# The first rows of a prefix log-sum-exp: found by Relu passes, or loaded apart

## The chip, the cores and the metric

The kernel runs on one core of a Trainium2 chip. The metric is device time in microseconds of one launch: 1260.91 us as the median of three runs before the change (1260.88 to 1261.64). One further execution was recorded by the hardware profiler; its span is 1258.4 us, from the first to the last instruction. The engines of the core are called PE (TensorE, matmul), ACT (ScalarE, activation functions), DVE (VectorE), POOL (GpSimd) and SP (SyncE, which here issues transfers). Sixteen DMA engines move the data between the memory of the chip and the core's own buffers.

## What is computed

The input is `x` of shape (4, 4096, 4128), float32, drawn from a normal distribution. For each of the 4 batches and 4128 columns, the output at row t is the logarithm of the sum of exp over rows 0 to t:

```
out[:, 0, :] = x[:, 0, :]
for t in range(1, S):
    mx = max(out[:, t-1, :], x[:, t, :])
    out[:, t, :] = mx + log(exp(out[:, t-1, :] - mx) + exp(x[:, t, :] - mx))
```

270.5 MB are read and as many are written.

## The kernel before, in words

The kernel computes exp, running sums and log without the running maximum. This is exact enough as long as the values are moderate. A check that runs along decides at the end whether they were; if not, a slow general loop (`_general`) does everything again. The check has two parts. Each batch's last sum must not be too large (`probe`, at most 2^62). And the first rows must not be too small, since a first row alone has no other term to hold its sum away from zero: this part is what changes.

**Steps.** A batch's 4096 rows are cut into steps of 128 x r rows, r being 2 or 3 (`begin`, `usual`, `final`, lines 149 to 151). Partition p of a step holds r consecutive rows of 4128 columns. There are 49 steps, numbered through all batches; 13 belong to batch 0 and 12 to each of the others. They use four buffers in turn (`slots`), one of two rows and three of three. A load moves 4128 or 6192 KB, a store the same.

**Chunks.** A step's columns are cut into three chunks of 1376 (`CH`). For each chunk:

- `exp` (line 102): Exp in place over all r rows, on ACT. At the first step of a batch a second pass follows (line 105): Relu of (2^-63 - exp(x)) over row 0, one partition, whose sum along the row goes into one element of `short`. The sum is over zero if a value is smaller than 2^-63.
- `sums` (lines 114 and 116): DVE adds the rows of a partition, into `z`.
- `head` (line 124): PE multiplies `z` by a triangular matrix (`below` at a batch's first step, `carried` after it), so that each partition gets the sum of those above it.
- `add` (lines 133, and 141 or 136): DVE adds this to the rows. In the last step of a batch the `z` pass also writes a column of `probe`.
- `log` (lines 146 and 147): Ln in place, on ACT.

**Order.** Each engine has a list written out by hand: ACT takes the three Exps of step 0, then for each chunk the two Ln passes of step t and an Exp of step t + 1; DVE and PE follow suit. `moves` is the list of SP, which issues all 98 loads and stores: four loads, store 0, store 1, load 4, store 2, load 5 and so on. A load waits for the store that last used its buffer, a store for the step's Ln passes, and each stands in SP's queue behind the transfer before it. An engine executes its list in order.

**Completion counters.** Each transfer that SP or ACT issues adds to one of eight completion counters, which the framework deals out in turn, in the order in which it has put the transfers; whoever needs the data waits on the counter. SP's and ACT's transfers share these eight. A transfer that takes a counter again waits, in the queue of the engine that issues it, until that counter's last transfer has landed. In the program before, SP is the only issuer (but for `_general`), and eight transfers back is always long done.

**The begin.** POOL clears and builds the small constants (lines 44 to 65) and clears `z` (line 69). ACT loads its function table (line 34).

**The end.** Lines 236 to 251 fill `fits`, 1 where a value is in bounds: 12 columns for `probe`, then 12 in which partition 0 takes the comparison of `short`. DVE takes the minimum along each partition (`low`), PE sums over the partitions (`good`), DVE compares with 128 and writes `flag`, which every engine then loads and branches on (lines 254 and 255).

Of the kernel before, what the change touches and what calls it, by code (L numbers as in the profile page):

```python
# [7 lines left out]
FP32 = mybir.dt.float32  # L8
I32 = mybir.dt.int32
ACT = mybir.ActivationFunctionType  # L10
ALU = mybir.AluOpType
AX = mybir.AxisListType
P = 128
MM = 512
NC = 3
SLOTS = 4
SMALL = 2.0 ** -63
LARGE = 2.0 ** 62


# [1 line left out]
def kernel(  # L22
# [5 lines left out]
    nc = tc.nc  # L28
    B, S, D = x.shape
    assert S % P == 0 and D % (NC * 32) == 0  # L30
    CH = D // NC
# [3 lines left out]
    consts = ctx.enter_context(tc.tile_pool(name="consts", bufs=1))  # L35
# [10 lines left out]
        out=below, in_=below, pattern=[[1, P]], compare_op=ALU.is_ge,  # L46
# [5 lines left out]
        out=carried, in_=below, pattern=[[0, P]], compare_op=ALU.not_equal,  # L52
# [5 lines left out]
    probe = consts.tile([P, B * NC], FP32, name="probe")  # L58
    nc.gpsimd.memset(probe, 1.0)

    short = consts.tile([1, B * NC], FP32, name="short")
    spare = consts.tile([1, CH + 8], FP32, name="spare")[:, :CH]
    tiny = consts.tile([1, 1], FP32, name="tiny")
    nc.gpsimd.memset(short, 0.0)
    nc.gpsimd.memset(tiny, SMALL)

    z = [zpool.tile([P, CH], FP32, name=f"z{c}") for c in range(NC)]
    for t in z:
# [2 lines left out]
    slots = [x2.tile([P, 2, D], FP32, name="x0")]  # L71
    slots += [x3.tile([P, 3, D], FP32, name=f"x{k}") for k in range(1, SLOTS)]
    sides = [ppool.tile([P, CH], FP32, name=f"p{k}") for k in range(2)]

    ctx_sched = tc.manual_schedule()
    ctx_sched.__enter__()
# [16 lines left out]
    class Chunk:  # L93
# [3 lines left out]
            self.cols = slice(c * CH, (c + 1) * CH)  # L97

        def exp(self):
            t = self.t  # L100
            e = t.xt[:, :, self.cols]
            nc.scalar.activation(e, e, ACT.Exp)  # L102
            if t.first:
                k = t.b * NC + self.c
                nc.scalar.activation(  # L105
                    spare, t.xt[0:1, 0, self.cols], ACT.Relu, bias=tiny, scale=-1.0,
                    accum_out=short[:, k:k + 1],
                )

        def sums(self):  # L110
            r = self.t.r
# [108 lines left out]
    done, at = set(), {e: 0 for e in lists}  # L220
    while any(at[e] < len(l) for e, l in lists.items()):
        before = len(done), sum(at.values())
        for e, l in lists.items():
            while at[e] < len(l):
                op = l[at[e]]
# [7 lines left out]
        assert before != (len(done), sum(at.values()))  # L233


    fits = consts.tile([P, 2 * B * NC], FP32, name="fits")
    nc.vector.memset(fits[:, B * NC:], 1.0)
    nc.vector.tensor_scalar(
        out=fits[:, :B * NC], in0=probe, scalar1=LARGE, scalar2=None, op0=ALU.is_le,
    )  # L240
    nc.vector.tensor_scalar(
        out=fits[0:1, B * NC:], in0=short, scalar1=0.0, scalar2=None, op0=ALU.is_le,
    )
    low = consts.tile([P, 1], FP32, name="low")
    nc.vector.tensor_reduce(out=low, in_=fits, op=ALU.min, axis=AX.X)  # L245
# [4 lines left out]
        out=flag, in0=good, scalar1=float(P), scalar2=None, op0=ALU.is_lt,  # L250
# [62 lines left out]
```

## Time and profile before

| What | us |
|---|---|
| median of three runs | 1260.91 |
| span of the profiled execution | 1258.4 |
| DVE busy | 956.2 (76%) |
| ACT busy | 955.4 (76%) |
| PE busy | 602.4 (48%) |
| ACT waiting for loads (line 102) | 219.7, 43 times |
| DVE waiting for ACT's Exp (line 114) | 216.5, 35 times |
| load, issue to landing: 3 rows, 2 rows (median) | 38.4, 33.0 |
| store, issue to landing: 3 rows, 2 rows (median) | 25.0, 21.6 |

The profiled execution is one of its own; its span of 1258.4 us lies 2.5 us under the median, since the span counts from the first to the last instruction. The page shows busy time by engine, then the span cut into 40 slices of 31.5 us with each engine's busy share in tenths, the share of time that the DMA engines were at work, and the rate. A group line names the source line, the engine, the operation and its operands, the count, then busy time and mean duration in ns, then the idle time ahead of it. A time line gives the start, the duration, the engine, the line, and in brackets how long the engine sat idle before and what ended that. A row of busy time by stretches gives the stretch, its length, then busy time and count for PE, its weight loads, DVE, ACT and POOL, then the granted clock of PE, the share of the DMA engines' time that packets took (by the packets that start in the stretch, so that it can exceed 1), and GB/s.

### The profile page before, as it was taken

Reading aid. Unit: us, or ns where it says so; the run is one execution under the profiler, and the core shown is the slowest. Engines: PE = TensorE matmul, PEld = TensorE weight load, DVE = VectorE, ACT = ScalarE, POOL = GpSimd, SP = SyncE. Lnnn points to the kernel's source line nnn. Section 1 sums busy time; section 2 is a strip of 40 time slices with the busy share of each in tenths; the row PEclk is TensorE's granted clock in tenths of the full one; section 3 lists DMA queues with packets and bytes.
Section 4 is the critical chain, followed back from the end, with each engine's and each line's share of the span. In section 5 each row is a group of like instructions: output and inputs, shape, how many; then the busy total and the mean of one; then the engine's idle time right before and its main releaser. Section 6 shows DMA issues by size and latency. Waiting matters only on the chain.

```text
span 1258.4 us, 3228 instructions
## 1 busy us (share of the span) xinstructions
PE 602.4 (48%) x884; PEld 233.1 (19%) x884; DVE 956.2 (76%) x548; ACT 955.4 (76%) x466; POOL 4.6 (0%) x14
## 2 busy tenths in 40 slices
PE   3654454453535455345364535634535553463361
PEld 1221121121212122112121212211211211121120
DVE  3997696795967699579596679957957976795792
ACT  6987687786976699578697668866968966896792
POOL 1000000000000000000000000000000000000000
PEclk9877776676677667666676666766766776676676
DMA  9999999999999999999999999999999999999998
GB/s 403 420 439 426 432 436 428 432 437 429 439 425 438 430 437 433 436 435 427 440 422 436 436 432 434 434 430 435 437 428 437 431 435 431 434 437 433 432 435 354
DMA packets 14131, 541.28 MB, mean 430 GB/s; under 512 B 1568, under 2 KB 1568, under 8 KB 1568
## 3 DMA queue, kind: packets, MB, share of 16 engines
q1 hardware_dynamic: 14112, 541.07, 99.6%
q8 instruction: 7, 0.11, 0.0%
q14 instruction: 12, 0.10, 0.0%
HBM read 270.53 MB, written 270.53 MB: 430 GB/s over the span
## 4 chain that ended last, share of the span: by engine, by line
DMA 69%; ACT 14%; DVE 13%; PE 1%; issue 1%; SPq 0%; ACTq 0%; DVEq 0%
DMA x<-in_x_dram 52%; DMA out_dram<-x 17%; ACT x L102 6%; DVE x L133 5%; ACT x L146 5%; DVE z L116 3%; ACT x L147 3%; DVE z L141 3%; DVE x L114 2%; PE p L124 1%; SPq L91 0%; DVE z L136 0%; ACTq L146 0%; ACTq L254 0%; SPq L88 0%
## 5 line engine op out<-in xcount | busy, mean ns | idle before, releaser
L124 PE MATMUL p<-z,carried 128*128 128x512 f32 (+1 forms) x810 | 551.8, 842 | 544.3 <-DVE z L116 544.3
L102 ACT ACTIVATE x<-x 128x4128 f32<-128x4128 f32 (+1 forms) x147 | 468.0, 3187 | 219.7 <-DMA x<-in_x_dram 219.7
L124 PEld LDWEIGHTS p<-z,carried 128*128 128x128 f32 x810 | 213.4, 280 | 882.2 <-DVE z L116 648.3
L133 DVE TENSOR_TENSOR x<-p,x 128x2752 f32<-128x2752 f32 (+1 forms) x147 | 361.9, 2462 | 6.2 <-PE p L124 6.2
L146 ACT ACTIVATE x<-x 128x2752 f32<-128x2752 f32 (+1 forms) x147 | 300.6, 2045 | 63.5 <-DVE z L141 58.5
L114 DVE TENSOR_TENSOR x<-x 128x1376 f32<-128x1376 f32 x90 | 142.9, 1588 | 216.5 <-ACT x L102 216.5
L116 DVE TENSOR_TENSOR z<-x 127x1376 f32<-127x1376 f32 x147 | 233.9, 1591 | 53.8 <-ACT x L102 49.4
L141 DVE TENSOR_TENSOR z<-x 128x1376 f32<-128x1376 f32 x135 | 215.0, 1592 | 4.6
L147 ACT ACTIVATE x<-z 128x1376 f32<-128x1376 f32 x147 | 196.0, 1334 | 0.0
L124 PE MATMUL p<-z,below 128*128 128x512 f32 (+1 forms) x72 | 50.4, 864 | 87.4 <-DVE z L116 87.4
L124 PEld LDWEIGHTS p<-z,below 128*128 128x128 f32 x72 | 19.6, 289 | 117.7 <-DVE z L116 78.8
L136 DVE CUSTOM_DVE_ANT_0 z<-x 128x1376 f32<-128x1376 f32 x12 | 19.1, 1592 | 0.4
L105 ACT ACTIVATE spare<-x,tiny 1x1376 f32<-1x1376 f32 x12 | 17.3, 1442 | 0.5
L69 POOL MEMSET z<- 128x1376 f32 x3 | 3.7, 1241 | 0.0
L105 ACT ACTIVATION_READ_ACCUMULATOR spare<-x,tiny 1x1 f32 x12 | 2.2, 186 | 0.0
L247 PE MATMUL good<-ones,low 128*1 128x1 f32 x2 | 0.2, 164 | 3.8 <-DVE low L245 3.8
L34 ACT ACT_TABLE_LOAD x1 | 1.3, 1283 | 0.8 <-PEq L297 0.8
L136 DVE DVE_READ_ACCUMULATOR2_ANT probe<- 128x1 f32 x12 | 1.0, 83 | 0.0
L247 PEld LDWEIGHTS good<-ones,low 128*1 128x1 f32 x2 | 0.1, 80 | 4.8 <-DVE low L245 4.8
L249 DVE TENSOR_SCALAR flag<-good 1x1 int32<-1x1 f32 x1 | 0.1, 148 | 0.3 <-PE good L247 0.3
L51 POOL TENSOR_SCALAR_AFFINE_SELECT carried<-below 128x128 f32<-128x128 f32 x1 | 0.3, 290 | 0.0
L45 POOL TENSOR_SCALAR_AFFINE_SELECT below<-below 128x128 f32<-128x128 f32 x1 | 0.3, 285 | 0.0
(13 smaller groups left out, 1.6 us busy)
## 6 DMA issues: line engine op xcount, KB each, us to landing
x<-in_x_dram SPq DMA_DIRECT2D x30, 6192.0 KB, 38.4
out_dram<-x SPq DMA_DIRECT2D x30, 6192.0 KB, 25.0
x<-in_x_dram SPq DMA_DIRECT2D x19, 4128.0 KB, 33.0
out_dram<-x SPq DMA_DIRECT2D x19, 4128.0 KB, 21.6
```

Source lines behind the costliest of these rows:

```text
L34: nc.scalar.preload_act_table_set("natural_log_exp_and_others")
L69: nc.gpsimd.memset(t, 0.0)
L102: nc.scalar.activation(e, e, ACT.Exp)
L105: nc.scalar.activation(spare, t.xt[0:1, 0, self.cols], ACT.Relu, bias=tiny, scale=-1.0, accum_out=short[:, k:k + 1],)
L114: nc.vector.tensor_tensor(out=e[1], in0=e[0], in1=e[1], op=ALU.add)
L116: nc.vector.tensor_tensor(out=self.z[0:n], in0=e[r - 2][0:n], in1=e[r - 1][0:n], op=ALU.add,)
L124: nc.tensor.matmul(pt[:, a:b], lhsT=w, rhs=self.z[:, a:b], start=True, stop=True,)
L133: nc.vector.tensor_tensor(out=e, in0=base, in1=e, op=ALU.add)
L136: nc.vector.tensor_tensor_reduce(out=self.z, in0=ends[0], in1=ends[1], scale=1.0, scalar=0.0, op0=ALU.add, op1=ALU.add, accum_out=probe[:, ...
L141: nc.vector.tensor_tensor(out=self.z, in0=ends[0], in1=ends[1], op=ALU.add)
L146: nc.scalar.activation(e, e, ACT.Ln)
L147: nc.scalar.activation(t.xt[:, r - 1, self.cols], self.z, ACT.Ln)
```

## The change

The Relu passes and their tiles (`short`, `spare`, `tiny`) go. In their place, a tile `firsts` of 16 partitions, nine blocks of 129 numbers wide, is cleared by POOL at the begin and filled by 14 loads that ACT issues, ahead of everything else that ACT does but its table load. A batch's first row of 4128 numbers is 32 pieces of 129 numbers (516 bytes); the 14 loads take 2 to 15 such pieces each, one piece to a partition, and are packed into the blocks. At the end DVE takes the least value of each of the 16 partitions of `firsts`, and `fits` gets one column in which these are compared with -43. The tile is made 245 numbers wider than it is used. Exp's own passes, the steps, the lists and all loads and stores of SP stay as they are.

```diff
-SMALL = 2.0 ** -63
+LOWEST = -43.0
+ROWS = 16
+BLOCKS = 9
+PIECE = 129
+PAD = 245
+PARTS = [[15, 14, 3], [13, 12, 7], [11, 10, 9, 2], [8, 6, 5, 13]]
...
-    short = consts.tile([1, B * NC], FP32, name="short")
-    spare = consts.tile([1, CH + 8], FP32, name="spare")[:, :CH]
-    tiny = consts.tile([1, 1], FP32, name="tiny")
-    nc.gpsimd.memset(short, 0.0)
-    nc.gpsimd.memset(tiny, SMALL)
+    firsts = consts.tile([ROWS, BLOCKS * PIECE + PAD], FP32, name="firsts")[:, :BLOCKS * PIECE]
+    nc.gpsimd.memset(firsts, 0.0)
...
+    used = [0] * BLOCKS
+    for b, sizes in enumerate(PARTS):
+        assert sum(sizes) * PIECE == D
+        at = 0
+        for k in sizes:
+            g = next(g for g in range(BLOCKS) if used[g] + k <= ROWS)
+            nc.scalar.dma_start(
+                out=firsts[used[g]:used[g] + k, g * PIECE:(g + 1) * PIECE],
+                in_=x[b, 0, at * PIECE:(at + k) * PIECE].rearrange("(p f) -> p f", f=PIECE),
+            )
+            used[g] += k
+            at += k
...
-            if t.first:
-                k = t.b * NC + self.c
-                nc.scalar.activation(
-                    spare, t.xt[0:1, 0, self.cols], ACT.Relu, bias=tiny, scale=-1.0,
-                    accum_out=short[:, k:k + 1],
-                )
...
-    fits = consts.tile([P, 2 * B * NC], FP32, name="fits")
+    fits = consts.tile([P, B * NC + 1], FP32, name="fits")
...
+    least = consts.tile([ROWS, 1], FP32, name="least")
+    nc.vector.tensor_reduce(out=least, in_=firsts, op=ALU.min, axis=AX.X)
     nc.vector.tensor_scalar(
-        out=fits[0:1, B * NC:], in0=short, scalar1=0.0, scalar2=None, op0=ALU.is_le,
+        out=fits[0:ROWS, B * NC:], in0=least, scalar1=LOWEST, scalar2=None, op0=ALU.is_ge,
     )
```

More of the change, by code (lines that the diff above doesn't have):

```diff
@@ L99, in exp @@
         def exp(self):
-            t = self.t
-            e = t.xt[:, :, self.cols]
+            e = self.t.xt[:, :, self.cols]
             nc.scalar.activation(e, e, ACT.Exp)
-            if t.first:
-                k = t.b * NC + self.c
-                nc.scalar.activation(
-                    spare, t.xt[0:1, 0, self.cols], ACT.Relu, bias=tiny, scale=-1.0,
-                    accum_out=short[:, k:k + 1],
-                )
         def sums(self):
```

## The prediction

> **What bounds the kernel now.** I read the page's head and its DMA rows first.
>
> ```profile
> span 1258.4 us, 3228 instructions
> DVE  3997696795967699579596679957957976795792
> ACT  6987687786976699578697668866968966896792
> DMA  9999999999999999999999999999999999999998
> q1 hardware_dynamic: 14112, 541.07, 99.6%
> DMA 69%; ACT 14%; DVE 13%; PE 1%; issue 1%; SPq 0%; ACTq 0%; DVEq 0%
> ```
>
> ACT (ScalarE) and DVE (VectorE) are each 76% busy and have room in every slice; the 16 DMA engines have none in any. The one queue q1 moves 541.07 MB in the 1258.4 us, and its packets fill 99.6% of the engines' time. ACT and DVE appear in the chain of waits because a load that comes before its ACT pass is a step of that chain; that does not mean they limit the rate. The busy time by stretches says where DMA time is lost (last two columns: mean busy share of the DMA engines, GB/s):
>
> ```profile
> 0.00:12.00 12.00, 0.00 (x0) 0.00 (x0) 0.00 (x0) 1.28 (x1) 4.64 (x14) 1.00 0.87 352
> 12.00:47.60 35.60, 21.56 (x38) 8.95 (x39) 27.32 (x18) 33.87 (x23) 0.00 (x0) 0.90 1.01 424
> 100.00:1180.00 1080.00, 517.76 (x741) 199.24 (x739) 828.57 (x464) 820.01 (x390) 0.00 (x0) 0.67 1.00 433
> 1250.00:1258.40 8.40, 0.00 (x0) 0.00 (x0) 0.00 (x0) 0.00 (x0) 0.00 (x0) 0.50 0.35 150
> ```
>
> From 12 to 1250 us nothing is lost; 541.07 MB at 433 GB/s are 1249.6 us, so only 1258.4 - 1249.6 = 8.8 us lie around the saturated stream: start-up, a little below 433 GB/s early on, and an end in which the engines finish unevenly (share 0.35 over the last 8.4 us: 2.9 us of work for the mean engine, the rest is waiting for the last ones). The median of 1260.91 is 2.5 us above this span; I carry that 2.5 us over unchanged.
>
> **The passes that go.** 12 Relu passes on ACT, each with the read of its sum:
>
> ```profile
> L105 ACT ACTIVATE spare<-x,tiny 1x1376 f32<-1x1376 f32 x12 | 17.3, 1442 | 0.5
> L105 ACT ACTIVATION_READ_ACCUMULATOR spare<-x,tiny 1x1 f32 x12 | 2.2, 186 | 0.0
> ```
>
> 17.3 + 2.2 = 19.5 us of ACT time, three passes (4.9 us) at the first step of each batch. For batches 1 to 3 they lie inside the stretch where the DMA share is 1.00: stores would be issued some us sooner into a queue that still has a transfer running. Gain 0. The cover is the transfer in flight: SP stands a whole transfer ahead there (in one first step the ACT stream runs on from the Relu at 641.4, and the next pass that waits for a load starts at 647.0). For batch 0 the time line shows what follows:
>
> ```profile
> 13.07 2.50 ACT L102 ACTIVATE x<-x 128x2752 f32<-128x2752 f32 x1 [10.99 <-DMA x<-in_x_dram]
> 15.67 1.44 ACT L105 ACTIVATE spare<-x,tiny 1x1376 f32<-1x1376 f32 x1
> 22.35 1.59 DVE L133 TENSOR_TENSOR x<-p,x 128x1376 f32<-128x1376 f32 x1 [1.06 <-PE p L124]
> 25.60 1.35 ACT L146 ACTIVATE x<-x 128x1376 f32<-128x1376 f32 x1 [0.49 <-DVE z L141]
> 38.04 15.04 SPq L91 DMA_DIRECT2D out_dram<-x  x2
> 58.05 0.34 SPq L88 DMA_DIRECT2D x<-in_x_dram  x1
> ```
>
> The first Ln at 25.60 waits for DVE, DVE for PE's six matmuls from 17.41, and these for the first Exp alone. Without Relu the Exps end at 20.5 instead of 23.6, ACT idles until 25.6, and store 0 still goes out at 38.04. Gain 0 again. So all 19.5 us become ACT idle time: **0**.
>
> **The loads that come.** 14 loads, 128 rows of 516 bytes, 0.066 MB. By bytes, 0.066 MB / 433 GB/s = 0.15 us. By packets, no row shows one of 516 bytes. The page's instruction queue moved 12 packets beside the big ones in the trace: an 8192-byte one took 0.31 us (27 bytes per ns, so no visible fixed part), the 4-byte ones 0.01. So 0.02 to 0.1 us each, 8 on the mean engine and at most 14 on one (a load in which that engine has a share): 0.15 to 1.4 us, of which only what falls on the engine that ends last counts, so the low end is 0. I take **0.3**, near the byte rate, since the 8192-byte row already runs at it.
>
> The page DMA: Bandwidth & Descriptors of the Trainium skill (section "Why a DMA increments its semaphore by 16 and not by 1") says that a load from SP or ACT runs on the lowest-numbered k engines, k the largest divisor up to 16 of the slowest dimension. By it, k would be the partition count here, engine 0 would get 14 packets and engine 15 none, and the bound of 1.4 is right; with 8 on each it would be 0.8 and the low end 0.15. No row of before tells the engines apart.
>
> **What the loads delay.** ACT issues them ahead of its first Exp. They wait for GpSimd's clear of the new tile (16x1161; by the 1376-wide clear of 1.24 us, 1.05 us, ending near 2.1, no later than ACT's table load at 2.08). SP's four issues in a row took 1.91 us, 0.48 each, so 14 take 6.7 us: 2.1 + 6.7 = 8.8, ahead of 13.07 when load 0 lands. That alone costs nothing. But SP's and ACT's transfers share eight completion counters in turn, and one that takes a counter again waits, in its own engine's queue, for that counter's last transfer. If load 0 has the first turn, the eighth small load takes load 0's counter: ACT then stands until 13.07 and issues seven more, 7 x 0.48 = 3.3 us (by SP's shortest issue, 0.34: 2.4; by its longest, 0.54: 3.8), before the first Exp. Everything behind that Exp shifts by 3.3. Store 0: 38.04 + 3.3 = 41.3, while loads run until about 47. Store 1: its last Ln ends at 52.71, issued then; 52.7 + 3.3 = 56.0, first packet 1.0 us after the issue (as load 0: issue 0.80, first packet 1.81 in the packet records) at 57.0. Store 0 lands at 58.0 (load 4 at 58.05 waits for just that), its last packets are read near 57.4. Not dry: 0.4 us to spare. Load 4 still follows store 0's landing. By 100 us ACT waits for loads again and the shift is gone. Bounds: 0 with no shift; with 0.65 us per issue (twice SP's shortest) the shift is 4.6 and 0.9 us are lost. I take **0.4**. SP's loads 1 to 3 also take counters that small loads had: those land by about 9 and 16 us, and the queue has load 0 until 12, load 1 until 22: 0.
>
> **The end.** VectorE gains a minimum over 16x1161; by its 1376-wide adds (1.59 us) about 1.35 us, behind the last add:
>
> ```profile
> 1237.10 0.08 DVE L136 DVE_READ_ACCUMULATOR2_ANT probe<- 128x1 f32 x1
> 1237.30 0.15 DVE L241 TENSOR_SCALAR fits<-short 1x12 f32<-1x12 f32 x1
> 1237.95 0.15 DVE L249 TENSOR_SCALAR flag<-good 1x1 int32<-1x1 f32 x1 [0.28 <-PE good L247]
> 1239.89 0.33 SPq L91 DMA_DIRECT2D out_dram<-x  x1
> ```
>
> Nothing but the flag is queued behind it: flag at 1239.5 instead of 1238.1, under the last store's 17 us. **0**; without that cover 1.4.
>
> Sum: 0 + 0.3 + 0.4 + 0 = 0.7; span 1259.1, time 1260.91 + 0.7 = **1261.6**. Its own range: 1259.4 (the uneven end falls better by 1.5) to 1263.3 (both bounds, 1.4 + 0.9, and 0.1).
>
> **Rivals.**
>
> *A long hold of ACT at the start* (slower). If the turns fall otherwise (load 1 ahead of the small loads), a small load takes load 1's counter and ACT stands until load 1 lands, 22.8 us. With three more issues the first Exp is at 24.2, shift 11.2. Store 0: issued 49.2, first packet 50.2, queue dry since 47.2: 3.0 lost. Store 1: issued 63.9, first packet 64.9, store 0 through by 50.2 + 9.8 = 60.0: 4.9 lost. Load 4 stands behind store 1 on SP. Together 7.9 to 8 us: 1269.5 with the packets. It decides from a shift of 3.7 us on (57.4 - 1.0 - 52.7); each us past that costs about one. For it: 10.99 us of ACT wait already sit there, and ACT runs with no idle from 25.6 to 61, so nothing makes a delay good before the first stores. Against: 8.8 us of issue fit before 13.07 if loads are only issued.
>
> *Each small load waits for the one before it.* Issue to first packet is 1.0 us, a big packet ahead on the engine 1.2: 2.2 us each, 14 x 2.2 = 31, first Exp at 33, shift 20. Store 0 starts at 58.8 (11.6 dry), store 1 at 73.5 against 68.6 (4.9): 1277.7. Against it: a counter is free again after seven other transfers. Chance 0.02. The same page ("Rules for kernel authors") calls transfers under 64 KB mostly overhead, and its fit has about 2.0 us fixed for each; its estimate for 14 in line, 28 us, comes out near this, and no run here shows such a load yet.
>
> *The engines finish more evenly* (faster). The last stretch has share 0.35 over 8.4 us: even finishing would end at 1250 + 2.9 = 1252.9 plus the 1.3 us between last landing and end of span (landing records: 1257.1). 1254.2 is -4.2; two thirds of it gives 1258.1. For it: the spread, 0.5 us at the first landing and 5.6 at the last, comes from packets that ran long on one engine or another, which another start can shuffle. Against: nothing in the change aims at the slow engines, and added packets can also fall on them (+1.5).
>
> *ACT's 19.5 us come back in the time*: 1241. The saturated stream alone needs 1249.6. 1 in 100.
>
> *The check misfires* and the slow loop runs: the smallest first-row value of normal numbers lies far above -43, the cleared rest of the tile is 0. No chance worth a number.
>
> **How the numbers follow.** Forecast 0.45; long hold, in all its sizes from a shift of 3.7 on, 0.31; small loads in line 0.02; evener end 0.21; the 19.5 us 0.01. The bound that a measurement of this kernel can tell from no change is 0.2%, 2.5 us: 1258.4 to 1263.4. Faster: the evener end's better part and the last rival, 0.19. Slower: the hold's larger sizes (0.28), small loads in line (0.02) and an end that falls worse (0.06), 0.36. Same: 0.45. Range 1257.8 to 1269.5: one in ten is left below and one above.
>
> **What would show it.** Right: no L105; first Exp at about 16.4; first Ln near 29; store 0 near 41; DMA share 1.00 from 12 to 1250; q1's share unchanged beside 128 small packets of another queue; the flag near 1239.5. Wrong: the first Exp at 13.07 (no shared turn), or past 17; DMA shares below 0.95 between 44 and 70 us; ACT no less busy than before minus 19.5 us; a last landing later or earlier than store 49's issue explains.

## The result, and the profile after

The changed kernel takes 1264.47 us, median of eight runs (1264.24 to 1266.37), beside 1260.89 for eight runs of the kernel before: a ratio of 1.003, with a 95% interval of 1.002 to 1.004. It is slower by 3.6 us. The profiled execution has a span of 1263.1 us, 4.7 above the span before. In the runs that have both figures the time is 1.7 to 1.8 us above the span, so the profiled execution of before lay some 0.7 us under its median by this, and the profiled pair lies further apart than the medians; the medians are what counts.

The head and the DMA rows of the page after:

```profile
span 1263.1 us, 3230 instructions
ACT  3987687685876699578686669857866876896692
DMA  8999999999999999999999999999999999999998
q1 hardware_dynamic: 14112, 541.07, 99.4%
q10 hardware_dynamic: 256, 0.07, 0.0%
```

One digit of the DMA row differs from before: the first slice has 8 where it had 9. ACT's busy time fell from 955.4 to 937.8 us. The new queue q10 has 256 packets for 128 rows of 516 bytes, so each data packet has a 4-byte one beside it, the count on the completion counter. That is the number that comes out if a load of k partitions runs on k engines and each of these counts once, as the Trainium skill has it (DMA: Bandwidth & Descriptors, "Why a DMA increments its semaphore by 16 and not by 1").

Busy time by stretches after, in the columns explained before (the last two are the busy share of the DMA engines and GB/s):

```profile
0.00:12.00 12.00, 0.00 (x0) 0.00 (x0) 0.00 (x0) 1.28 (x1) 5.55 (x13) 1.00 0.91 351
12.00:47.60 35.60, 19.44 (x33) 8.23 (x34) 24.35 (x16) 26.15 (x15) 0.00 (x0) 0.87 0.94 396
100.00:1180.00 1080.00, 528.29 (x744) 204.39 (x744) 828.69 (x465) 804.98 (x371) 0.00 (x0) 0.66 1.00 433
12.00:52.00 40.00, 23.25 (x41) 9.73 (x42) 28.57 (x19) 30.55 (x18) 0.00 (x0) 0.87 0.93 382
12.40:16.00 3.60, 0.00 (x0) 0.00 (x0) 0.00 (x0) 0.00 (x0) 0.00 (x0) 1.00 0.47 127
```

The last two stretches in the kernel before:

```profile
12.00:52.00 40.00, 23.58 (x43) 9.69 (x43) 31.45 (x21) 38.27 (x26) 0.00 (x0) 0.91 1.00 423
12.40:16.00 3.60, 0.00 (x0) 0.00 (x0) 0.33 (x1) 2.83 (x2) 0.00 (x0) 1.00 1.02 440
```

The long stretch from 100 to 1180 us is as it was, 433 GB/s. From 12 to 47.6 us the rate is 396 instead of 424 GB/s: 28 x 35.6 = 1.0 MB not moved, 2.3 us at 433 GB/s. This cut flatters the changed kernel: the kernel before has a slow piece of its own from 44 to 48 us (330 GB/s, with the engines busy), and the changed kernel has its like only from 48 to 52 us (297 GB/s). Up to 52 us, where both have it, the rate is 382 instead of 423 GB/s: 1.6 MB or 3.8 us, about the whole loss. The row from 12.4 to 16 us says where most of it lies: the engines move 127 GB/s there. Before, the same 3.6 us had 440 GB/s, so 1.1 MB or 2.6 us are missing in this hole alone. The time line shows who was late:

```profile
0.80 0.39 SPq L103 DMA_DIRECT2D x<-in_x_dram  x1
14.76 1.78 SPq L103 DMA_DIRECT2D x<-in_x_dram  x3
2.10 14.48 ACTq L83 DMA_DIRECT2D firsts<-in_x_dram  x14
16.63 7.27 ACT L116 ACTIVATE x<-x 128x2752 f32<-128x2752 f32 x3 [14.54 <-DMA firsts<-in_x_dram]
41.16 15.04 SPq L106 DMA_DIRECT2D out_dram<-x  x2
SPq L103 <- DMA firsts<-in_x_dram: 14.1, 2, 13.6
```

SP issues load 0 at 0.80 as before, and then nothing until 14.76; before, all four loads were out at 2.7. The last line is from SP's own waits: 13.6 us in one wait for a load of `firsts`. Load 1 has the sixteenth turn of the eight counters (load 0, then 14 small loads), so it takes the counter of the seventh small load and must see that one land. By then load 0's 128 packets are through, and the engines have nothing but small packets. ACT's first Exp is late too (16.63 instead of 13.07), since the eighth small load takes load 0's own counter.

At the end, the new minimum is in its place and hidden:

```profile
1240.81 0.08 DVE L144 DVE_READ_ACCUMULATOR2_ANT probe<- 128x1 f32 x1
1241.01 1.34 DVE L250 TENSOR_REDUCE least<-firsts 16x1 f32<-16x1161 f32 x1
1243.01 0.15 DVE L259 TENSOR_SCALAR flag<-good 1x1 int32<-1x1 f32 x1 [0.28 <-PE good L257]
1243.60 0.33 SPq L106 DMA_DIRECT2D out_dram<-x  x1
```

### The profile page after: what moved, and what is told of

Read it like the earlier page. It is cut to its first block, busy times and chain, and to the rows that moved or that the text cites. A ratio compares the mean times of both kernels' runs of the same rounds, so it can differ in the third digit from the quotient of the medians.

```text
span 1263.1 us, 3230 instructions
## 1 busy us (share of the span) xinstructions
PE 611.6 (48%) x884; PEld 237.7 (19%) x884; DVE 957.3 (76%) x549; ACT 937.8 (74%) x442; POOL 5.6 (0%) x13
## 4 chain that ended last, share of the span: by engine, by line
DMA 69%; ACT 15%; DVE 12%; issue 1%; PE 1%; SPq 0%; ACTq 0%; DVEq 0%
DMA x<-in_x_dram 52%; DMA out_dram<-x 17%; ACT x L116 7%; ACT x L154 5%; DVE x L141 5%; ACT x L155 3%; DVE z L124 3%; DVE z L149 3%; DVE x L122 2%; PE p L132 1%; DVE z L144 0%; SPq L106 0%; ACTq L83 0%; ACTq L154 0%; SPq L103 0%
## 5 line engine op out<-in xcount | busy, mean ns | idle before, releaser
L132 PE MATMUL p<-z,carried 128*128 128x512 f32 (+1 forms) x810 | 562.9, 856 | 539.2 <-DVE z L124 539.2
L132 PEld LDWEIGHTS p<-z,carried 128*128 128x128 f32 x810 | 218.4, 287 | 884.2 <-DVE z L124 645.3
```

Source lines behind the costliest of these rows:

```text
L132: nc.tensor.matmul(pt[:, a:b], lhsT=w, rhs=self.z[:, a:b], start=True, stop=True,)
```

## The experiments

Theory: the loss is the dry stretch of the DMA engines that SP's wait for a counter makes. Rivals: the small packets cost time on the engines; ACT's late first Exp costs; the removal of the Relu passes costs. All times are medians beside runs of the kernel before on the same chip; the intervals are of the ratio.

### The same rows in 4, 7, 8 and 10 loads

The number of loads ahead of load 1 decides whose counter load 1 takes; the bytes stay the same. Each load has 16 partitions.

```diff
-PARTS = [[15, 14, 3], [13, 12, 7], [11, 10, 9, 2], [8, 6, 5, 13]]
+PARTS = [[32]] * 4                                   # 4 loads
+PARTS = [[32], [16, 16], [16, 16], [16, 16]]         # 7 loads
+PARTS = [[16, 16]] * 4                               # 8 loads
...
+            wide = k // ROWS
+            nc.scalar.dma_start(
+                out=firsts[:, g * PIECE:(g + wide) * PIECE],
+                in_=x[b, 0, at * PIECE:(at + k) * PIECE].rearrange("(p f) -> p f", f=wide * PIECE),
+            )
```

Here `g` counts the blocks that are filled so far. With 10 loads, two batches come in three loads of 16 x 86 and two in two of 16 x 129.

> The first rows come by 4 loads (16 partitions of 258 numbers each) instead of 14, on ScalarE's queue, no Relu passes. Theory (SP's second load stood until 14.76 us for a completion counter that a small load had, and the DMA engines ran dry): with load 0 and four small loads, load 1 takes the sixth counter, unused so far, and is issued right behind load 0; first Exp at 13.1 us; DMA share about 1 from 2 us on; 1260.9 +- 1. Rival 'the packets themselves': 64 data and 64 counter packets, half of the changed kernel's, so half of its loss: 1262.7. Rival 'ScalarE is held': no hold, 1260.9.

> 7 small loads on ScalarE's queue. Theory: load 1 gets the ninth turn, load 0's own counter, and waits for load 0 to land (13.3 to 14 us); first packet a us later, stream dry from 12.4: 2 to 2.6 us lost, 1263.2. ScalarE's queue has no wait in it: first Exp about 14. Rival 'the packets themselves': 112 data packets, 1264.0. Rival 'ScalarE is held': not held, 1260.9.

> 8 small loads on ScalarE's queue, one more than the run with 7. Theory: load 1 gets the tenth turn, the counter of the first small load, which lands near 9 us: issued about 9.1, ahead of the end of load 0 at 12.4, nothing lost: 1260.9 +- 1, faster than with 7 loads. ScalarE's eighth load waits for load 0: first Exp about 14. Rival 'the packets themselves': 128 data packets as in the changed kernel, slower than with 7: 1264.5. Rival 'ScalarE is held': one issue held, 1261.

> 10 small loads on ScalarE's queue (128 + 32 packets: two batches in three loads of 16 x 86, two in two of 16 x 129). Theory: SP's load 1 gets the twelfth turn, the counter of the third small load; with 8 loads the first landed at 9.1 and the second at 12.0, so the third lands near 13.7, after load 0's stream has ended near 13: first packet at 14.7, 1.7 lost against the run with 8: 1264. Rival 'number of loads or packets': a little over the run with 8, 1262.4; and below the run with 7 (1265.2) only by chance.

| small loads | load 1's counter had | SP issues load 1 at | time, us | above before | ratio, interval |
|---|---|---|---|---|---|
| 4 | no one | in a row with load 0 | 1262.45 | 1.65 | 1.0013, 1.0004 to 1.0022 |
| 7 | load 0 | 14.45 | 1265.15 | 4.35 | 1.0035, 1.0023 to 1.0048 |
| 8 | small load 1 | 9.12 | 1262.17 | 1.37 | 1.0010, 1.0001 to 1.0019 |
| 10 | small load 3 | 14.02 | 1263.98 | 3.31 | 1.0026, 1.0016 to 1.0036 |
| 14 (the change) | small load 7 | 14.76 | 1264.47 | 3.58 | 1.003, 1.002 to 1.004 |

The order 8, 10, 7 is that of load 1's issue and not that of the number of loads: with 7 loads the kernel is 3.0 us slower than with 8. The issues with 8 loads, with 10 and with 7, then the rate between 12.4 and 16 us in each, in that order:

```profile
9.12 3.25 SPq L103 DMA_DIRECT2D x<-in_x_dram  x2
...
12.40:16.00 3.60, 0.00 (x0) 0.00 (x0) 0.00 (x0) 1.36 (x1) 0.00 (x0) 1.00 1.07 420
```

```profile
14.02 1.30 SPq L99 DMA_DIRECT2D x<-in_x_dram  x3
...
12.40:16.00 3.60, 0.00 (x0) 0.00 (x0) 0.00 (x0) 0.49 (x1) 0.00 (x0) 1.00 0.54 154
```

```profile
14.45 1.29 SPq L103 DMA_DIRECT2D x<-in_x_dram  x3
...
12.40:16.00 3.60, 0.00 (x0) 0.00 (x0) 0.00 (x0) 1.54 (x1) 0.00 (x0) 1.00 0.53 156
```

420 GB/s where load 1 goes out at 9.12, 154 and 156 where it goes out at 14: the hole comes with the late issue. The issue at 9.12 is the landing of the first small load, and load 2, at 12.04, that of the second. So they land 2.9 us apart, though ACT issued them within half a us. What the numbers do not say is why 7 loads lose 0.8 us more than 14, with load 1 issued 0.3 us sooner; the intervals overlap, and the two profiled executions took the same, 1264.87 and 1264.88 us. And 4 and 8 loads, with no hole, still lose 1.4 to 1.7 us: the expectation of 1260.9 missed here, so there is a second cost. (With 4 loads the row from 12.4 to 16 us has a share of 0.82, but a share goes by the packets that start in the stretch; in the packet records the engines are never idle there and move 370 GB/s.) The rival of the packets came nearer with 4 loads, 1262.7 for 1262.45; but with 8 loads and twice the packets it called for 1264.5, and 1262.17 came. With 7 loads, 2 to 2.6 us were expected and 4.35 came, about the hole and this second cost together.

### GpSimd as the issuer

```diff
-            nc.scalar.dma_start(
+            nc.gpsimd.dma_start(
```

> The same 14 loads with the same parts, issued by GpSimd, whose transfers have counters of their own, so that neither SP nor ScalarE waits for one. Theory: load 1 issued right behind load 0, first Exp at 13.1, DMA share near 1 from 2 us on: 1261 +- 1. Rival 'the packets themselves': 128 data packets as in the changed kernel, 1264.5. Rival 'ScalarE is held': 1260.9.

1261.60 against 1260.80, ratio 1.0007 (0.9998 to 1.0016). The same 14 parts, off the shared counters, bring the loss from 3.6 down to 0.8, which cannot be told from nothing. SP's four loads go out in a row from 0.81, and the first Exp starts at 13.33. The run changes a second thing too: GpSimd issues from 6.16 us on and waits between its own loads from the ninth on, so the small packets start at 10.0 instead of 6.1 us and are spread until 46 us.

### The same 14 loads later

```diff
             nc.scalar.activation(t.xt[:, r - 1, self.cols], self.z, ACT.Ln)
+            if self.c == NC - 1 and t.n >= 2 and small:
+                into, of = small.pop(0)
+                nc.scalar.dma_start(out=into, in_=of)
```

> The same 14 loads with the same parts on ScalarE's queue, but one after the last Ln of each step from step 2 to step 15, so that SP's first four loads have the first four turns. Theory: first Exp at 13.1, no dry stretch at 12 to 16 us; the small packets may stretch big ones by some tenths of a us: 1261 to 1262. Rival 'the loads as such cost what the changed kernel lost': 1264.5.

1260.77 against 1260.72, ratio 1.000 (0.9991 to 1.0009). Fourteen loads of the same parts, on ACT's queue, without a Relu pass, cost nothing that shows once the begin is over; the interval is 1.1 us to either side. The loss is one of the begin and not of the loads as such. This is the best form of the change found, and it equals the kernel before; it does not beat it.

### The Relu passes alone

```diff
-            if t.first:
-                k = t.b * NC + self.c
-                nc.scalar.activation(
-                    spare, t.xt[0:1, 0, self.cols], ACT.Relu, bias=tiny, scale=-1.0,
-                    accum_out=short[:, k:k + 1],
-                )
```

> The kernel before without its 12 Relu passes and with no small loads: it leaves the check of the first rows out (its column in fits stays at the clear's value). Theory (the stream of the DMA engines sets the time): ScalarE idles 19.5 us more and the time stays at 1260.8 +- 0.7. Rival 'the 19.5 us come back': 1241. If the removal of the Relu passes has a part in the changed kernel's loss, it is above 1262 here.

1260.78 against 1260.72, ratio 1.000 (0.9991 to 1.0009). 19.5 us less work on an engine that is 76% busy, and the medians lie 0.06 us apart, with an interval of 1.1 us to either side.

### ACT's first Exp late, and nothing else

```diff
+            if t.n == 0 and self.c == 0:
+                for _ in range(3):
+                    nc.scalar.activation(spare, t.xt[0:1, 0, self.cols], ACT.Relu)
             nc.scalar.activation(e, e, ACT.Exp)
```

The second run has 8 in place of 3.

> The kernel before, with three Relu passes over one row, of no use, ahead of the first Exp: that Exp starts at 13.1 + 3 x 1.5 = 17.6, a shift of 4.5, later than the 16.6 of the changed kernel, while SP's four loads go out in a row. Theory (ScalarE's late start is hidden up to a shift of 3.7, each us past that costs one): 0.8 lost, 1261.6. Rival 'the late first Exp is what costs': more than the changed kernel's loss, 1265 or above.

> As the run with three useless passes, but with eight: first Exp near 25, a shift of 12. Theory: store 0 issued near 50, the stream dry from 47.2 to 51 (3.8 lost), store 1 issued near 64.7, first packet 65.7 against 60.8 (4.9 lost): 8.7 lost, 1269.5. Rival 'the late first Exp costs one for one': 1272.8. Rival 'the stream makes good for it': 1261.

With three passes the first Exp starts at 17.25, 0.6 us later than in the changed kernel, and the time is 1262.66 against 1260.72 (1.0014, 1.0005 to 1.0023): 1.9 lost, where 0.8 was expected. Its rows from 64 to 80 us say what the expectation lacked:

```profile
64.00:70.00 6.00, 2.46 (x5) 1.01 (x5) 4.59 (x4) 6.00 (x4) 0.00 (x0) 0.78 1.01 380
70.00:80.00 10.00, 7.68 (x11) 2.73 (x10) 9.90 (x7) 7.97 (x5) 0.00 (x0) 0.60 0.97 370
```

The engines are busy in both, but move 380 and 370 GB/s where the kernel before moves 440 and 423. The hole ahead of store 1 is there too, and small (share 0.82 from 56 to 60 us). With eight it starts at 24.23, and the time is 1269.63 (1.007, 1.0056 to 1.0083): 8.9 lost, 8.7 expected. The stream with eight passes:

```profile
49.21 15.04 SPq L91 DMA_DIRECT2D out_dram<-x  x2
44.00:51.00 7.00, 5.83 (x9) 2.19 (x8) 6.78 (x5) 7.00 (x5) 0.00 (x0) 0.55 0.44 189
60.00:66.00 6.00, 4.96 (x10) 1.83 (x9) 5.73 (x4) 6.00 (x4) 0.00 (x0) 0.85 0.26 110
```

Two holes, ahead of store 0 and ahead of store 1, where the prediction's arithmetic had put them. In the changed kernel this hold has no hole to make: load 1 is itself 4 us late, so the stream has loads until about 51 us, and store 0 (issued at 41.16) is in time; by the packet records its engines are never idle from 40 to 70 us. A shift under the threshold of 3.7 us was not run by itself.

### What the second cost is

One load for all four rows, then the four loads on SP's own queue behind its load 3.

```diff
+    nc.scalar.dma_start(                                   # one load
+        out=firsts[:, :8 * PIECE].rearrange("p (b f) -> p b f", b=B),
+        in_=x[:, 0, :].rearrange("b (p f) -> p b f", p=ROWS),
+    )
```

```diff
             nc.sync.dma_start(out=self.xt, in_=self.dram(x))
+            if self.n == SLOTS - 1:
+                firsts_in()                                # four loads, nc.sync.dma_start
```

> One load for all four first rows (16 partitions of 4 x 258 numbers, 64 packets of 1032 bytes) on ScalarE's queue at the begin. No counter is taken again before SP's fourth load. The runs with 4 and 8 lost 1.4 us without a dry stretch, their big packets 0.2 us longer while small ones ran between them. If that goes with the number of small packets on an engine: 4 here as with 4 loads, 1262.3. If with the number of loads: a quarter of 1.7, 1261.2. If with the first meeting of two queues alone: 1262.3 as well, and with big packets long until 20 us.

> The 4 loads of the run with 4, but on SP's own queue behind its fourth load: same packets, no second queue; no counter is taken again before store 0, which takes load 0's, long landed. Theory that two queues on one engine stretch the big packets: none here, 1260.8. Rival that the reads of the first rows do it: 1262.

One load: 1262.48 against 1260.67 (1.0010, 1.0001 to 1.0019), as much as four or eight. Four loads on SP's queue: 1260.89 (1.0001, 0.9992 to 1.0010), nothing. The stretch from 16 to 44 us with one load on ACT's queue, then with four on SP's:

```profile
16.00:44.00 28.00, 17.30 (x31) 7.20 (x32) 22.31 (x15) 22.73 (x14) 0.00 (x0) 0.94 1.00 407
```

```profile
16.00:44.00 28.00, 18.32 (x33) 7.88 (x34) 23.69 (x16) 22.91 (x14) 0.00 (x0) 0.91 1.01 436
```

The engines are busy in both, share 1.00 and 1.01, but move 407 GB/s in one and 436 in the other: busy with packets that take longer. In the packet records with one load, the 33,024-byte packets take 1.22 us from 3 to 6 us, on average 1.39 to 1.53 from 7 to 25 us, long after the last small packet (13.6 us), and 1.23 again from 27 us on (373 GB/s from 20 to 30 us against 429 before). So the second cost is not a price for each small packet or load. It comes where small loads of another queue run between the packets of load 0. SP's four loads differ from that in two things at once: their queue, and their time, since they run behind load 3, at 47 to 48 us. So whether the second queue or the early time makes the cost is not separated. How the packets get longer, no run here shows; the slow pieces before (44 to 48 us) and with three useless passes (64 to 80 us), also with busy engines, have one queue only. Nor does the cost come in every execution: with one load, four of eleven took 1260.5 to 1260.9 us, no more than the kernel before, and the others 1262.2 to 1263.8; the profiled one, at 1262.99, is one of the latter.

## Why the prediction was right or wrong

**Right.** The DMA stream sets the time: without the Relu passes it does not move (1260.78). The end is hidden: minimum 1.34 us against 1.35, the flag ahead of the last store. The begin of ACT: clear of the tile 1.06 us against 1.05, the eighth small load waits for load 0, first Exp at 16.63 (16.4 forecast), first Ln at 28.72 ("near 29"), store 0 at 41.16 ("near 41"). It comes out this well partly by two errors against each other: load 0 landed at 14.05 instead of 13.07, and the seven issues behind it took 2.53 us instead of 3.3. The arithmetic of the long hold is confirmed by the run with eight useless passes, 8.9 lost against 8.7; close to its threshold it fell short, 1.9 against 0.8 with three.

**Wrong.** The likeliest case was no change (1261.6), and the kernel is slower by 3.6 us; 1264.47 lies within the range given and outside the likeliest case's own 1259.4 to 1263.3. The step that failed is the sentence on SP: "SP's loads 1 to 3 also take counters that small loads had: those land by about 9 and 16 us, and the queue has load 0 until 12, load 1 until 22: 0." The wait was seen and priced at nothing, because the small loads were given a landing soon after their issue, all at once. Behind a full stream they land one after another: on each engine the data packet of a small load takes its turn behind a big packet of 1.22 us, and its 4-byte count takes another turn behind the next, so 2 x 1.22 = 2.4 us for each load by this count, and 2.9 apart by the issues of the run with 8. In the packet records of the changed kernel the data packets of small load 1 start from 6.11 us and its counts from 7.36, those of small load 2 from 8.58 and 9.82. The Trainium skill has the turns (DMA: Bandwidth & Descriptors, "Queues, rings and completion order": an engine goes round the queues that have work). The trace agrees: 1.22 to 1.25 us, one big packet, lie between these starts. By the landing records small load 1 is in at 9.07 us and small load 2 at 11.93, and small loads 3 to 7 from 13.86 to 14.74. Seven in a row behind a first one at 9 cannot land by 12; they land when load 0 is through and the engines are idle, at 14.74. The term for SP, 0, is 2.2 us in the time by the difference to the run with 8 loads (3.6 - 1.4). The prediction's own sign for it, a DMA share of 1.00 from 12 us on, failed with 0.94 from 12 to 47.6 us.

**Mis-sized.** "I take 0.3" for the packets, with a bound of 1.4. The runs without a hole lose 1.4 (8 loads), 1.7 (4) and 1.8 (1). The bound was nearly right by chance: it was made of a price for each packet, and the cost does not go with packets.

**The hold of ACT**, 0.4 in the sum and the place of the slower rival: its mechanism exists (the hold, the threshold), but in the changed kernel it is not what decides. The rival that came true is a relative of it, a wait for the same shared counters on the other queue. The even end did not come: engines still finish 6 us apart in the landing records.

**Small slips of the working.** Twice SP's shortest issue of 0.34 is 0.68 and not 0.65, which makes the bound of the hold 1.1 instead of 0.9. The 1269.5 of the long hold adds its 7.9 to the forecast, which holds the short hold's 0.4 already. And "room in every slice" is more than the row shows: DVE has the digit 9, 90% or more, in several slices. None of them touches the step that failed.

## What to carry to other kernels

Where transfers of two queues share a few completion counters, a handful of small loads put in front of a big stream can hold the stream's own next load: count the turns, see whose counter each big transfer takes, and ask when that one lands behind a full queue rather than on an idle one. A small load cost nothing that showed here when it was issued behind the first big loads, by SP itself or some steps later, where eight turns back was long done. And work taken from an engine that the stream already hides is not a gain to be set against such a risk.

## What the hardware showed that was not expected

Packets of 516 bytes take only 0.03 us in the records, but a small load landed 2.9 us after the one before it while a full stream ran on the same engines. And one load of 66 KB on a second queue at the begin left 33,024-byte packets about 0.2 us longer for some 18 us in the profiled execution (407 GB/s from 16 to 44 us instead of 439), while the same rows on the stream's own queue at 47 us, or 14 loads on the second queue from 71 us on, left no mark in the time.
